# Tables without a scratch tile, angles one unit sooner, and an earlier load of x in a state-space layer on one core

## The chip, the cores and the metric

The kernel runs on one NeuronCore of a Trainium2 chip, in one launch. The metric is the device time of one execution in microseconds (us); the time of a kernel is the median of its runs. Engines are called PE (matrix), PEld (its weight loads), DVE (vector), ACT (scalar, activation functions), POOL (GpSimd) and SP (the queue that issues nearly all transfers here).

## The reference, cut to what matters

The program is one step of a decoder trunk: a state-space (S5) layer with a gated output, a convolutional FFN, a shared K/V projection, a differential attention layer and a second FFN, for a prompt of 1024 tokens and 8 x 8 sample tokens. The change lies in the first layer alone:

```
def s5_mixer(u, h0, lam_re, lam_im, log_dt, b_re, b_im, c_re, c_im, d_skip, w_glu):
    lam_dt = lam * dt;  lam_bar = exp(lam_dt);  b_bar = ((lam_bar - 1) / lam) * b
    # per group g (64 of them, 16 channels, 64 complex states), per token:
    #   h = lam_bar * h + b_bar @ u ;  y = real(c @ h)
    z = gelu(y + d_skip * u)
    gl = z @ w_glu
    return gl[..., :D] * sigmoid(gl[..., D:]), h_last
...
x = x + rmsnorm(s5_mixer(rmsnorm(x, a_pre_g), ...), a_post_g)
```

## The kernel before

**Layout.** `s5` cuts the 1024 tokens into 128 rows of 8 consecutive tokens. The recurrence inside a row is a product with small tables; between rows it is a real first-order scan over 128 steps on DVE, after the phase of each state was turned away by a table of cosines and sines. The 64 groups are handled in 8 blocks of 8 groups, each block in units of 3, 3 and 2 groups: 24 units, k = 3b + i for block b.

**Preparation** (L199 to L411, in a pool `s5prep`; its order on each engine is chosen by the framework's planner). It loads the parameters, b and c, transposes b, c and the powers of lambda (`bt`, `ct`, `NT`) with PE into the layouts `Yt` and `Dt`, and reads all of x (`xj`, eight transfers of 512 KB through four buffers) only to get the row norms: an ACT Square with a sum for each, then `rstd_from` on DVE, then `rs`.

**The block loop** is written out by hand (`tc.manual_schedule()`, L635 on): every engine runs its instructions in the order of the program text. The pieces are generators, and `run(...)` advances each by one stage:

- `load(b)`: x of one block into `zk` (three buffers); `scale(b)`: eight ACT multiplications by `rs` into `xg`, in two stages.
- `tables(b)`: six DVE operations on 128x1024 in three stages, which make `gn`, `cl` and `cw`; before, one product goes through a scratch tile `ax`. Two transfers follow (`cw<-cl`).
- `angles(q)`: for the two blocks 2q and 2q+1, three DVE operations on the same tile `ax` (stage 1), then ACT's Abs and three Sin and six transfers between partition halves (stage 2); the results are `cosT` and `sinT` of the two blocks. `ax` has one buffer. A tile is written again only when the readers of its former content, transfers among them, are done.
- `lags(b)`: 16 small products, four ACT copies, two POOL operations and seven transfers (L514) into `M1`.
- `turn(k)` and `states(k)`: PE transposes, POOL and ACT copies, 12 matmuls; `factors(k)`: one ACT copy into `Rs`; `scan(k)`: seven DVE operations that need `cosT`, `sinT`, `Rs` and the matmuls' PSUM; `out(k)`: PE products with `M1`, `cl`, `cw`; `gelu(k)`: ACT, and a store; `z_out(b)`: 8 PE transposes, two ACT casts and two DVE subtractions (L630) into the `xT_hi` and `xT_lo` of the dense part.

In step k the loop issues turn(k+2), the first stage of z_out, out(k), the products of lags, states(k+2), scan(k+1), the rest of z_out, gelu(k), factors(k+2), load, and then the stages of tables, scale and angles for later blocks. After the loop `then()` opens the dense part, which begins with the GLU's weights (`raw<-in_glu_w_dram`).

Of the kernel before, what the change touches and what calls it, by code (L numbers as in the profile page):

```python
# [20 lines left out]
P = 128  # L21
# [52 lines left out]
def trunk_kernel(ctx, tc, I, O):  # L74
# [7 lines left out]
    def nm(s):  # L82
        uid[0] += 1
        return f"{s}_{uid[0]}"
# [79 lines left out]
    def s5(then):  # L164
        with ExitStack() as c5:
# [33 lines left out]
            with tc.tile_pool(name="s5prep", bufs=1, reuse_waits="tile") as pr:  # L199

                def pt(shape, tag, dtype=F32):
                    return pr.tile(shape, dtype, tag=tag, name=tag)
# [13 lines left out]
                ht = pt([P, 4, 2, S], "ht")  # L216
                nc.sync.dma_start(adn[:, 0], I["a_pre_g"][0].rearrange("(g c) -> g c", c=C))
                nc.sync.dma_start(adn[:, 1], I["ssm_d"][0].rearrange("(g c) -> g c", c=C))
                for s, b_ in enumerate(("ssm_b_re", "ssm_b_im")):
                    nc.sync.dma_start(bt[:, s], I[b_][0])  # L220
                for s, c_ in enumerate(("ssm_c_re", "ssm_c_im")):
                    nc.sync.dma_start(ct[:, :, s, :], I[c_][0])
                for s, h_ in enumerate(("state_ssm_re", "state_ssm_im")):
                    nc.sync.dma_start(ht[:, :, s, :], I[h_][0].rearrange("(q b) g p -> (b g) q p", b=2))

                nc.sync.dma_start(gr, I["a_pre_g"][0].rearrange("(g c) -> g c", c=C).partition_broadcast(P))
                sq = pt([P, D], "sq", BF16)
                s1 = pt([TS, 1], "s1")
                A.activation(sq[0:TS], xs, AF.Square, accum_out=s1)

                r = rstd_from(pr, s1, 1, TS, "r1")
                A.mul(xs, xs, r[0:TS])
# [113 lines left out]
                    V.tensor_scalar(EX[:, 2, h], sn[q, 8], -1.0 if h == 0 else 1.0, None, op0=ALU.mult)  # L346
                    GP.tensor_copy(EX[:, 3, h], ph8[q])

                ss = pt([P, L], "ss")
                for j in range(L):  # L350
                    xj = pr.tile([P, D], F32, tag="xj", name=nm("xj"), bufs=4)
                    nc.sync.dma_start(xj, xp[:, j])
                    A.activation(sq, xj, AF.Square, accum_out=ss[:, j : j + 1])
                r = rstd_from(pr, ss, L, P, "r")
                GP.tensor_copy(rs, r)

# [79 lines left out]
            def angles(q):  # L436


                x = bt_("ax", 1)
                (t, sr), (t1, s1) = trig[2 * q], trig[2 * q + 1] = [[bt_(n, 3) for n in ("cosT", "sinT")]  # L440
                                                                    for _ in range(2)]
                V.tensor_tensor(x, bc(PH[:, q], 2, NCH), bc(kk, 1, BG), ALU.mult)
                V.tensor_scalar(t, x, MAGIC, None, op0=ALU.add)
                V.scalar_tensor_tensor(x, t, MAGIC, x, op0=ALU.subtract, op1=ALU.subtract)
                yield
                A.activation(t, x, AF.Abs)
                A.activation(sr, x, AF.Sin, scale=-TWO_PI)
                A.activation(x, x, AF.Sin, scale=TWO_PI)
                A.activation(t, t, AF.Sin, bias=halfpi, scale=-TWO_PI)
                lo, hi = slice(0, 64), slice(64, 128)  # L450
                for dst, i, src, j in ((t1, lo, t, hi), (t1, hi, t, hi), (s1, lo, sr, hi), (s1, hi, x, hi),
                                       (t, hi, t, lo), (sr, hi, x, lo)):
                    nc.sync.dma_start(dst[i], src[j])
                yield
# [16 lines left out]
            def tables(b):  # L471

                gs = slice(b * BG, (b + 1) * BG)

                def tb(w):
                    return Dt[:, w, :, gs].rearrange("p j g -> p g j").unsqueeze(3).broadcast_to([P, BG, L, C])

                def yb(w):
                    return Yt[:, w, gs].unsqueeze(2).broadcast_to([P, BG, L, C])

                gn, t = bt_("gn"), bt_("ax", 1)
                V.tensor_tensor(v4(gn), yb(0), tb(0), ALU.mult)
                V.tensor_tensor(v4(t), yb(1), tb(1), ALU.mult)
                yield
                V.tensor_tensor(gn, gn, t, ALU.add)
                cl = bt_("cl")
                V.tensor_tensor(v4(cl), yb(2), tb(2), ALU.mult)
                blocks[b].append(gn)
                yield
                cw = bt_("cw")  # L490
                V.tensor_tensor(v4(cw), yb(3), tb(3), ALU.mult)
                V.tensor_tensor(cl, cl, cw, ALU.add)
                blocks[b] += cl, cw
                nc.sync.dma_start(cw[0:64], cl[64:128])
                nc.sync.dma_start(cw[64:128], cl[0:64])
                yield
# [138 lines left out]
            with tc.manual_schedule():  # L635
                def run(*gs):
                    for g in gs:
                        next(g, None)

                for b in range(3):  # L640
                    load(b)
                tab, sca, lag, ang = tables(0), scale(0), lags(0), angles(0)
                run(sca, sca, tab, tab, ang)
                turn(0)
                run(ang, tab)
                factors(0)
                states(0)
                run(lag, lag)
                tab = tables(1)
                run(tab)  # L650
                for k in range(-1, nun):

                    b, i = k // 3, k % 3
                    if k + 2 < nun:
                        turn(k + 2)
                    zo = z_out(b - 1) if i == 0 and b else iter(())
                    run(zo)
                    if k >= 0:
                        out(k)
                    if i == 1 and b + 1 < NBK:  # L660
                        lag = lags(b + 1)
                        run(lag)
                    if k + 2 < nun:
                        states(k + 2)
                    if k + 1 < nun:
                        scan(k + 1)
                    run(zo, zo)
                    if k >= 0:
                        gelu(k)
                    if k + 2 < nun:  # L670
                        factors(k + 2)
                    if i == 0 and b and b + 2 < NBK:
                        load(b + 2)
                    if i == 1 and b + 1 < NBK:
                        run(lag)
                        if b + 2 < NBK:
                            tab = tables(b + 2)
                            run(tab)
                    if i == 2 and b + 2 < NBK:
                        sca = scale(b + 2)  # L680
                        run(sca, tab)
                        if b % 2 == 0:
                            ang = angles(b // 2 + 1)
                            run(ang)
                    if i == 0 and b + 1 < NBK:
                        run(sca, tab)
                        if b % 2 == 1:
                            run(ang)
                for _ in z_out(NBK - 1):
                    pass  # L690
            c5l.close()
# [1323 lines left out]
```

## Time and profile before

| what | value |
|---|---|
| median of 3 runs | 2748.95 us (2748.61 to 2752.87) |
| the profiled execution's own time | 2752.58 us |
| its span, first to last instruction | 2750.8 us |
| mean granted clock of PE | 0.972 |
| busy: PE / DVE / ACT / POOL | 2528.7 / 1953.1 / 1255.9 / 692.9 us |

The span lies 1.8 us inside the profiled execution's time, and that execution is 3.6 us above the median. The state-space layer takes the first 245 us or so; the first GLU matmul starts at 250.34 us. The table's shares are averages over all stages; the stage of the change has limits of its own.

### The profile page before, as it was taken

To read this page: it belongs to the slowest core of one execution; us is meant where nothing else is said; L and a number is where in the kernel's file an instruction comes from. 1 tells how busy PE (TensorE), PEld (TensorE's weight loads), DVE (VectorE), ACT (ScalarE), POOL (GpSimd) and SP (SyncE) were. 2 spreads that over 40 slices of the span, in tenths; PEclk is the share of its full clock that TensorE was granted. 3 is DMA by queue.
4 is the path that set the end of the run, shared out by engine and by line. 5 is a ranking of instruction groups with operands and counts; after the bars stand their busy time and mean duration, and the time that the engine had idled before them with its cause. 6 is when DMAs were issued, how large, how long until landed. Compare 5 with 4: busy or idle time off the path is not lost.

```text
span 2750.8 us, 39548 instructions
## 1 busy us (share of the span) xinstructions
PE 2528.7 (92%) x14362; PEld 2215.9 (81%) x14362; DVE 1953.1 (71%) x3719; ACT 1255.9 (46%) x2472; POOL 692.9 (25%) x943
## 2 busy tenths in 40 slices
PE   5777997999999989999999799999699999998995
PEld 4666886899999977778777688887599999996774
DVE  6885229776666789985222688865877776779998
ACT  5563124444444453444322577753444444454332
POOL 2221000111222266510201322100021222237661
PEclk9989998999999999999999999999899999999998
DMA  6334213222222243344656333324312222233324
GB/s 157 78 94 101 61 54 108 77 74 72 72 72 72 77 130 90 109 136 167 202 170 203 87 93 93 95 90 153 107 64 72 73 79 73 72 108 100 100 86 146
DMA packets 258023, 279.69 MB, mean 102 GB/s; under 512 B 41836, under 2 KB 205988, under 8 KB 257828
## 3 DMA queue, kind: packets, MB, share of 16 engines
q1 hardware_dynamic: 253508, 264.90, 31.4%
q0 software_dynamic: 3232, 10.29, 1.7%
q8 instruction: 114, 1.87, 0.3%
q10 hardware_dynamic: 1088, 1.97, 0.2%
q14 instruction: 81, 0.66, 0.1%
HBM read 187.82 MB, written 68.58 MB: 93 GB/s over the span
## 4 chain that ended last, share of the span: by engine, by line
PE 66%; DVE 16%; DMA 6%; ACT 5%; issue 4%; POOL 2%; SPq 1%; DVEq 0%; ACTq 0%; POOLq 0%
PE mm L784 18%; PE mm L785 18%; PE mm L786 18%; PE mm L1357 2%; DVE acc L1368 2%; DVE S L1830 1%; DVE xT_lo L137 1%; DMA raw<-in_w_down_dram 1%; DVE wst L137 1%; PE mm L1858 1%; DMA gr<-gd 1%; ACT S L1834 1%; PE tr L832 1%; DVE xT_hi L137 1%; DMA sinT<-sinT 1%
## 5 line engine op out<-in xcount | busy, mean ns | idle before, releaser
L784 PE MATMUL mm<-xT_hi,whi 128*128 128x320 f32 (+1 forms) x1408 | 459.6, 328 | 5.8 <-ACT xT_hi L136 2.8
L785 PE MATMUL mm<-xT_lo,whi 128*128 128x320 f32 (+1 forms) x1408 | 456.4, 324 | 0.1
L786 PE MATMUL mm<-xT_hi,wlo 128*128 128x384 f32 (+1 forms) x1408 | 454.8, 324 | 0.0
L1146 POOL COPY cvo<-acc 128x2 f32<-128x2 f32 x88 | 158.9, 1805 | 678.2 <-ACT acc L1129 678.2
L784 PEld LDWEIGHTS mm<-xT_hi,whi 128*128 128x128 f32 x1408 | 265.3, 189 | 15.0 <-DVE acc L1112 9.6
L137 DVE TENSOR_TENSOR wlo<-raw,whi 128x1024 fp32r<-128x1024 f32 x88 | 107.5, 1222 | 236.4 <-PE mm L785 231.9
L785 PEld LDWEIGHTS mm<-xT_lo,whi 128*128 128x128 f32 x1408 | 266.1, 189 | 0.9 <-DVE xT_lo L137 0.9
L786 PEld LDWEIGHTS mm<-xT_hi,wlo 128*128 128x128 f32 x1408 | 265.8, 189 | 0.2
L1143 DVE SCALAR_TENSOR_TENSOR acc<-acc,cpar,acc 128x1104 f32<-128x1104 f32 x176 | 240.5, 1387 | 0.7 <-ACT acc L1141 0.5
L784 PE MATMUL mm<-whi,xT_hi 128*128 128x512 f32 x576 | 228.3, 401 | 4.1 <-ACT whi L767 4.1
L785 PE MATMUL mm<-wlo,xT_hi 128*128 128x512 f32 x576 | 229.0, 398 | 0.0
L786 PE MATMUL mm<-whi,xT_lo 128*128 128x512 f32 x576 | 228.4, 398 | 0.0
L136 ACT CAST whi<-raw 128x1024 fp32r<-128x1024 f32 x88 | 92.8, 1055 | 283.6 <-PE mm L786 265.3
L1368 DVE TENSOR_TENSOR acc<-mm,acc 128x512 f32<-128x512 f32 x279 | 183.9, 679 | 9.2 <-PE mm L786 8.7
L784 PE MATMUL mm<-acc,whi 128*128 128x384 f32 x528 | 178.6, 339 | 3.8 <-DVE acc L1106 1.9
L786 PE MATMUL mm<-acc,wlo 128*128 128x384 f32 x528 | 178.7, 339 | 0.0
L785 PE MATMUL mm<-acc,whi 128*128 128x384 f32 x528 | 178.6, 338 | 0.0
L784 PEld LDWEIGHTS mm<-whi,xT_hi 128*128 128x128 f32 x576 | 108.8, 189 | 33.6 <-ACT whi L767 4.4
L786 PEld LDWEIGHTS mm<-whi,xT_lo 128*128 128x128 f32 x576 | 108.6, 189 | 26.6 <-issue 0.9
L785 PEld LDWEIGHTS mm<-wlo,xT_hi 128*128 128x128 f32 x576 | 108.6, 189 | 26.0 <-issue 0.4
L1141 ACT ACTIVATE acc<-acc,cpar 128x1104 f32<-128x1104 f32 x88 | 115.5, 1314 | 30.4 <-DVE acc L1112 19.8
L1830 DVE CUSTOM_DVE_ANT_0 S<-mm,tb 128x512 f32<-128x512 f32 (+3 forms) x192 | 101.2, 552 | 29.4 <-PE mm L1828 26.0
(559 smaller groups left out, 6263.6 us busy)
## 6 DMA issues: line engine op xcount, KB each, us to landing
raw<-in_w_up_dram SPq DMA_DIRECT2D x88, 512.0 KB
gd<-acc SPq DMA_DIRECT2D x44, 552.0 KB
raw<-in_w_down_dram SPq DMA_DIRECT2D x44, 512.0 KB
gr<-gd SPq DMA_DIRECT2D x80, 256.0 KB
raw<-in_glu_w_dram SPq DMA_DIRECT2D x32, 256.0 KB
acc<-in_cache_k_dram SPq DMA_DIRECT2D x16, 512.0 KB
acc<-in_cache_v_dram SPq DMA_DIRECT2D x16, 512.0 KB
xj<-in_x_prompt_dram SPq DMA_DIRECT2D x8, 512.0 KB
```

The lines of the kernel that those rows point to most:

```text
L136: A.copy(hi_ap, ps_ap)
L137: V.tensor_tensor(lo_ap, ps_ap, hi_ap.bitcast(F32), ALU.subtract)
L784: PE.matmul(out, lh, rh, start=start, stop=False, **kw)
L785: PE.matmul(out, lh, rl, start=False, stop=False, **kw)
L786: PE.matmul(out, ll, rh, start=False, stop=stop, **kw)
L832: PE.transpose(ps[:, c * n : (c + 1) * n], y[:, c * P : (c + 1) * P], ident[0:n, 0:n])
L1141: A.activation(hc, hb[:, 2 : 2 + TG], AF.Identity, bias=cp[:, ft, 3:4], scale=cp[:, ft, 2:3])
L1143: V.scalar_tensor_tensor(hc, hb[:, tap : tap + TG], cp[:, ft, tap : tap + 1], hc, op0=ALU.mult, op1=ALU.add)
L1146: GP.tensor_copy(co[:, 0:2], hb[:, SEQ : SEQ + 2])
L1357: PE.matmul(pa[h], lt, wt[:, h * 512 : (h + 1) * 512], start=st and j == 0, stop=sp and j == len(seq) - 1)
L1368: V.tensor_tensor(a, ps, a, ALU.add)
L1830: V.tensor_tensor_reduce(S_[j][:, k0 : k0 + w], ps[:, 0:w], H["tb"][:, b0 : b0 + w], 0.125, -3e38, ALU.add, ALU.max, mx[:, j, c : c + 1])
```

## The change

Six things change, all in `s5`:

1. In the preparation the transfers of `xj` are issued ahead of b and c (four at once, four more as buffers come free), and the transfers of the sample states `ht` after them.
2. `tables` no longer uses `ax`: the second product goes into `cl`, is added to `gn`, and `cl` is then written by the third product. Stage 1 has one DVE operation instead of two, stage 2 three instead of two.
3. `angles(0)` works in halves: Abs into a buffer of `zk`, then for each half of the partitions one cosine, one transfer and two Sin that write both halves themselves; two transfers in all instead of six.
4. `angles(q)` for q > 0 starts one unit sooner (stage 1 in unit 1 of an even block, stage 2 in unit 2).
5. `z_out` and `load` of odd blocks come one unit later.
6. At the loop's start angles go ahead of tables and scale; `factors(0)` goes behind `lags(0)`; `load(2)` behind both.

```diff
+                xj = [pr.tile([P, D], F32, tag="xj", name=nm("xj"), bufs=4) for _ in range(4)]
+                for j in range(4):
+                    nc.sync.dma_start(xj[j], xp[:, j])
                 for s, b_ in enumerate(("ssm_b_re", "ssm_b_im")):
                     nc.sync.dma_start(bt[:, s], I[b_][0])
...
-                for s, h_ in enumerate(("state_ssm_re", "state_ssm_im")):
-                    nc.sync.dma_start(ht[:, :, s, :], I[h_][0].rearrange("(q b) g p -> (b g) q p", b=2))
...
+                ss = pt([P, L], "ss")
+                for j in range(L):
+                    if j >= 4:
+                        xj.append(pr.tile([P, D], F32, tag="xj", name=nm("xj"), bufs=4))
+                        nc.sync.dma_start(xj[j], xp[:, j])
+                    A.activation(sq, xj[j], AF.Square, accum_out=ss[:, j : j + 1])
+                for s, h_ in enumerate(("state_ssm_re", "state_ssm_im")):
+                    nc.sync.dma_start(ht[:, :, s, :], I[h_][0].rearrange("(q b) g p -> (b g) q p", b=2))
...
-                ss = pt([P, L], "ss")
-                for j in range(L):
-                    xj = pr.tile([P, D], F32, tag="xj", name=nm("xj"), bufs=4)
-                    nc.sync.dma_start(xj, xp[:, j])
-                    A.activation(sq, xj, AF.Square, accum_out=ss[:, j : j + 1])
...
+                lo, hi = slice(0, 64), slice(64, 128)
+                if q == 0:
+
+                    xa = bt_("zk", 3)
+                    A.activation(xa, x, AF.Abs)
+                    for i, tc_, ts in ((lo, t, sr), (hi, t1, s1)):
+                        A.activation(tc_[i], xa[i], AF.Sin, bias=halfpi[i], scale=-TWO_PI)
+                        nc.sync.dma_start(tc_[hi if i == lo else lo], tc_[i])
+                        A.activation(ts[lo], x[i], AF.Sin, scale=-TWO_PI)
+                        A.activation(ts[hi], x[i], AF.Sin, scale=TWO_PI)
+                        yield
+                    return
...
-                gn, t = bt_("gn"), bt_("ax", 1)
+                gn = bt_("gn")
                 V.tensor_tensor(v4(gn), yb(0), tb(0), ALU.mult)
-                V.tensor_tensor(v4(t), yb(1), tb(1), ALU.mult)
                 yield
-                V.tensor_tensor(gn, gn, t, ALU.add)
                 cl = bt_("cl")
+                V.tensor_tensor(v4(cl), yb(1), tb(1), ALU.mult)
+                V.tensor_tensor(gn, gn, cl, ALU.add)
                 V.tensor_tensor(v4(cl), yb(2), tb(2), ALU.mult)
...
-                for b in range(3):
+                for b in range(2):
                     load(b)
                 tab, sca, lag, ang = tables(0), scale(0), lags(0), angles(0)
-                run(sca, sca, tab, tab, ang)
+                run(ang, tab, ang, sca, tab, sca)
                 turn(0)
-                run(ang, tab)
-                factors(0)
+                run(tab)
                 states(0)
                 run(lag, lag)
+                factors(0)
+                load(2)
                 tab = tables(1)
-                run(tab)
+                run(tab, ang)
...
-                    zo = z_out(b - 1) if i == 0 and b else iter(())
+                    zo = z_out(b - 1) if i == b % 2 and b > 0 else iter(())
...
-                    if i == 0 and b and b + 2 < NBK:
+                    if i == b % 2 and b > 0 and b + 2 < NBK:
                         load(b + 2)
...
                             tab = tables(b + 2)
                             run(tab)
+                            if b % 2 == 0:
+                                ang = angles(b // 2 + 1)
+                                run(ang)
                     if i == 2 and b + 2 < NBK:
                         sca = scale(b + 2)
                         run(sca, tab)
                         if b % 2 == 0:
-                            ang = angles(b // 2 + 1)
                             run(ang)
                     if i == 0 and b + 1 < NBK:
                         run(sca, tab)
-                        if b % 2 == 1:
-                            run(ang)
```

## Rows read from the trace of the kernel before

**Rows 1.** Busy time of each engine in three stretches of the block loop, each of two blocks (from unit 2 of blocks 0, 2 and 4); the columns are the stretch, its length, busy us (and instructions) of PE, PEld, DVE, ACT and POOL, the granted clock of PE, the DMA share and GB/s.
```profile
77.11:126.23 49.12, 36.80 (x324) 31.78 (x323) 40.60 (x62) 30.16 (x73) 9.13 (x23) 0.90 0.37 91
126.23:175.90 49.67, 34.62 (x298) 30.61 (x301) 40.27 (x62) 28.88 (x68) 10.61 (x22) 0.86 0.37 89
175.90:225.84 49.94, 35.27 (x316) 30.26 (x310) 41.46 (x62) 30.02 (x72) 10.60 (x22) 0.90 0.33 79
```

**Rows 2.** What DVE waited for between 60 and 262 us: line, releaser, us in total, times, longest.
```profile
DVE ax L483 <- DMA sinT<-ax: 34.3, 4, 11.3
DVE za L570 <- PE mm L551: 1.0, 1, 1.0
```

**Rows 3.** The timeline of DVE in the first two blocks of the loop: start, us, instruction, and in brackets the idle time before it.
```profile
79.85 1.42 DVE L482 TENSOR_TENSOR gn<-Yt,Dt 128x1024 f32<-128x1024 f32 x1
...
82.33 0.55 DVE L570 TENSOR_TENSOR za<-mm,cosT 128x384 f32<-128x384 f32 x1
...
86.01 1.22 DVE L485 TENSOR_TENSOR gn<-gn,ax 128x1024 f32<-128x1024 f32 x1
...
88.29 1.22 DVE L442 TENSOR_TENSOR ax<-PH,kk 128x1024 f32<-128x1024 f32 x1
...
91.41 0.55 DVE L570 TENSOR_TENSOR za<-mm,cosT 128x384 f32<-128x384 f32 x1
...
95.09 1.11 DVE L630 TENSOR_TENSOR xT_lo<-tr,xT_hi 128x512 fp32r<-128x512 f32 x1
...
97.10 1.22 DVE L491 TENSOR_TENSOR cw<-Yt,Dt 128x1024 f32<-128x1024 f32 x1
...
99.50 0.42 DVE L570 TENSOR_TENSOR za<-mm,cosT 128x256 f32<-128x256 f32 x1
...
102.25 1.42 DVE L482 TENSOR_TENSOR gn<-Yt,Dt 128x1024 f32<-128x1024 f32 x1
111.06 1.23 DVE L483 TENSOR_TENSOR ax<-Yt,Dt 128x1024 f32<-128x1024 f32 x1 [7.39 <-DMA sinT<-ax]
```

**Rows 4.** The timeline of ACT in the same blocks: the last scaling of unit 2 of block 0, and the first and last operation of stage 2 of `angles(1)`.
```profile
84.00 1.28 ACT L467 ACTIVATE xg<-zk,rs 128x128 f32<-128x128 f32 x4
...
95.13 1.05 ACT L446 ACTIVATE cosT<-ax 128x1024 f32<-128x1024 f32 x1
...
99.53 1.13 ACT L449 ACTIVATE cosT<-cosT,halfpi 128x1024 f32<-128x1024 f32 x1
```

**Rows 5.** The timeline of SP's queue: the first and the last issue of the transfers of `angles(1)`.
```profile
100.89 1.52 SPq L453 DMA_DIRECT2D cosT<-cosT  x2
...
107.44 0.46 SPq L453 DMA_DIRECT2D sinT<-ax  x1
```

**Rows 6.** The timeline of PE in the same blocks: half of the transposes of z_out(0), the start of out(3), and the states(5) behind it.
```profile
84.95 0.60 PE L622 MATMUL tr<-ident,zk 128*128 128x128 f32 x4
...
88.65 0.46 PE L593 MATMUL mm<-M,U 128*128 128x128 f32 x2 [2.67 <-DMA M<-M]
...
92.98 0.73 PE L551 MATMUL mm<-U,M 128*128 128x136 f32 x4
```

**Rows 7.** PE in a short stretch behind that wait: stretch, length, busy us (instructions), granted clock, DMA share, GB/s.
```profile
90.00:92.00 2.00, 2.00 (x10) 0.50 0.00 0
```

**Rows 8.** The timeline of DVE at the end of the preparation and the start of the loop.
```profile
38.78 0.17 DVE L118 TENSOR_SCALAR rv<-ss 128x8 f32<-128x8 f32 x1 [2.50 <-ACT sq L353]
...
41.01 1.23 DVE L482 TENSOR_TENSOR gn<-Yt,Dt 128x1024 f32<-128x1024 f32 x1
...
45.69 1.42 DVE L442 TENSOR_TENSOR ax<-PH,kk 128x1024 f32<-128x1024 f32 x1
...
63.93 1.22 DVE L483 TENSOR_TENSOR ax<-Yt,Dt 128x1024 f32<-128x1024 f32 x1 [11.30 <-DMA sinT<-ax]
```

**Rows 9.** The timeline of ACT at the start of the loop.
```profile
42.31 2.44 ACT L467 ACTIVATE xg<-zk,rs 128x128 f32<-128x128 f32 x8 [3.09 <-POOL rs L355]
...
49.13 1.06 ACT L446 ACTIVATE cosT<-ax 128x1024 f32<-128x1024 f32 x1 [2.04 <-DVE ax L444]
...
53.57 1.49 ACT L509 COPY M<-mm 16x256 f32<-16x256 f32 x4
```

**Rows 10.** The timeline of PE in the preparation (first transposes of b, last transposes) and at the start of the loop.
```profile
9.76 0.34 PE L367 MATMUL mm<-ident,bt 64*128 64x64 f32 x1 [9.76 <-DMA bt<-in_ssm_b_im_dram]
...
32.73 3.67 PE L399 MATMUL mm<-ident,NT 64*128 64x64 f32 x32 [0.85 <-ACT NT L336]
...
44.81 0.90 PE L531 MATMUL tr<-ident,xg 128*128 128x128 f32 x3 [7.37 <-ACT xg L467]
...
47.02 1.70 PE L551 MATMUL mm<-U,M 128*128 128x136 f32 x6 [0.66 <-ACT M L539]
48.51 1.49 PE L553 MATMUL mm<-U,M 128*128 128x128 f32 x6
51.63 1.05 PE L505 MATMUL mm<-cl,gn 128*16 128x128 f32 x16 [1.63 <-DVE cl L492]
```

**Rows 11.** Two stretches of 1 us, while c is loaded and while x is loaded; the columns as in rows 1 (the last two are the DMA share and GB/s).
```profile
11.00:12.00 1.00, 1.00 (x10) 0.65 (x8) 0.96 (x7) 0.56 (x1) 0.58 (x3) 1.00 1.41 153
...
17.00:18.00 1.00, 1.00 (x8) 0.69 (x6) 1.00 (x3) 1.00 (x1) 0.00 (x0) 1.00 1.02 414
```

**Rows 12.** SP's queue in the preparation: the issue of the first three transfers of x.
```profile
10.78 1.38 SPq L352 DMA_DIRECT2D xj<-in_x_prompt_dram  x3
```

More of the change, by code (lines that the diff above doesn't have):

```diff
@@ L449, in angles @@
                 A.activation(t, t, AF.Sin, bias=halfpi, scale=-TWO_PI)
-                lo, hi = slice(0, 64), slice(64, 128)
                 for dst, i, src, j in ((t1, lo, t, hi), (t1, hi, t, hi), (s1, lo, sr, hi), (s1, hi, x, hi),
```

## The prediction

> **What bounds the kernel now.** I read the busy times by stretch first, then DVE's waits, then the timelines of single engines. The page puts PE at 92% of the whole span, but in the block loop it is not the limit: over two blocks of 49.1 to 49.9 us DVE is busy 40.3 to 41.5 us, PE 34.6 to 36.8, ACT 29 to 30 [rows 1]. DVE has one wait there that counts: L483 writes `ax`, and the transfers of `angles` still read it, 34.3 us in four waits [rows 2]. One is 11.3 us at the loop's start [rows 8]; the others sum to 34.3 - 11.3 = 23.0 us, 7.4 us of it in the first pair of blocks [rows 3]. From 79.85 to 103.7 us DVE has no gap. So the loop is bound by DVE plus one stall for two blocks, and a us saved here should reach the end: what follows is a chain of matmuls that starts when the loop is done.
>
> **The three stalls in the loop.** First, what taking `ax` out of `tables` gives alone. The tables' six operations stay six, of the same shape, so DVE's work is unchanged. Without the wait L483 would run at 103.7 and unit 6's scan would want `cosT` and `sinT` at 104.8; they land where `ax` came free, near 111.0. The wait would move to the scan and 1.1 us would be gained. The earlier `angles` must bring the rest. I set unit 2's scan to zero (77.1 us before; 2.7 us ahead of 79.85 [rows 3]). DVE costs from rows 3: a scan of three groups 3.7 (82.33 to 86.01), of two 2.75 (99.50 to 102.25); two table operations 2.3 to 2.4 (86.01 to 88.29, 97.10 to 99.50), so some 1.2 each and 3.4 for three; angles 3.1 (88.29 to 91.41); the split 2.0 (95.09 to 97.10). After the change the order is: scan 2.7, table 1.4, angles 3.1 (ends 7.2); scan, three tables (14.3); scan, two tables (20.4); scan 2.75, split 2.0, one table (26.5); and then unit 6's scan. Stage 2 of `angles` runs on ACT behind unit 2's scaling, which began at 84.0 and took 1.2 [rows 4], so from 85.2, which is 8.1; its four operations and one table load take 5.5 (95.13 to 100.66 [rows 4]), to 13.6. From ACT's end to the landing took 111.0 - 100.7 = 10.4 before, since the six issues wait for each other and end at 107.44 [rows 4, 5]. So the tables of angles land at 24.0 and are wanted at 26.5. The wait goes, with 2.5 us in hand: 23.0 us for the three.
>
> What is late next? PE's out(3) waited for `M1` until 88.65, 11.5 after `cl` was ready at 77.1, and states(5) came 4.3 later, at 92.98, done by some 94.5 [rows 6]: 17.4 on this scale, wanted by unit 5's scan at 20.4. In the next block `cl` is ready at 20.4, two casts for the moved split (2 us on ACT) may stand ahead of the four lag copies, and states(8) end near 20.4 + 17.4 + 2 = 39.8, wanted at 41.7. Stage 2 on ACT (8.1 to 13.6) falls where ACT's next gelu would wait for out(3), which ends near 15.9 [rows 6]. SP is held for 6.5 us by the angles' issues (100.89 to 107.44 [rows 5]), but from 13.6 on: behind them stand the store of a gelu and the `cw` transfers, whose `cl` comes at 20.4. The load of odd blocks goes to SP one unit later, ahead of `M1`'s issues; it waits only for transposes that PE has run by then. The moved split holds a PSUM buffer in the unit that also needs one for lags, so states(6) may start only when a cast, a gelu or a lag copy frees one. I allow 0.5 us for each of three odd blocks (the nearest row is the single wait of a scan for PE, 1.0 us [rows 2]; bounds 0 and 1.6, where the states would follow the split's last subtraction): -1.5.
>
> **The tail.** For the last odd block the split of block 6 comes in unit 22. Its eight transposes, two groups of 0.6 that overlap a little [rows 6], used to lie in PE's wait for `M1`; now they stand ahead of out(22): -1.0 us, hidden in nothing.
>
> **The start.** Before, DVE waited for the last Square, did the row norms (38.78 to 41.0) and began tables at 41.01 [rows 8]. With x first the norms are done early, and what ends last is PE's chain that starts with b: from 9.76 to 32.73 + 3.67 = 36.4, of which 0.85 was a wait for `NT` that an emptier ACT removes [rows 10]. DVE's last copy leaves with that end. But b now stands behind 2.1 MB of x. While x flowed the rate was 414 GB/s, while c flowed 153 [rows 11]; 2.1 MB at 414 are 5.1 us, an upper bound for the delay since b's own issue is hidden in it; the lower bound is the four issues alone, 4 x 0.46 = 1.8 [rows 12]. I take 4.0, nearer to the upper, because one queue carries all of them. So DVE begins angles at 36.4 - 0.85 + 4.0 = 39.5 (37.3 to 40.7).
>
> From there, in us after that start: angles 3.4 (45.69 to 49.13 [rows 8, 9]); Abs, one cosine and two Sin of about 1.05 each, to 7.6 (a Sin on half the partitions is not in the trace; I take the full price, since the free size is the same, and half of it would gain 1.6); scaling 2.4, to 10.0; transposes and copies 2.2 (44.81 to 47.02), to 12.2; states 3.0 (47.02 to 50.0), to 15.2; the 16 lag products 1.05 [rows 10] and four copies 1.5 [rows 9], to 17.7; then `factors(0)`, moved behind them, 0.4, to 18.1. Only then can unit 0's scan step run. The rest of that unit is 2.0, three tables 3.4: 23.5. Unit 1 needs the three Sin of the other half (to 21.3), copies (22.4) and states (25.3); its scan ends at 28.3, two tables at 30.7, and unit 2 starts at 31, when states(2) come behind out(0). Before, unit 2 started at 77.1. So 77.1 - (39.5 + 31) = 6.6 us gained. With PE quick throughout and half-price Sin the walk is 28, with another wait for PE 33: bounds 77.1 - 65.3 = 11.8 and 77.1 - 73.7 = 3.4.
>
> The Trainium skill, "DMA: Bandwidth & Descriptors", section "Queues, rings and completion order", says that on each DMA engine descriptors are consumed in ring order. By that rule b waits for all of x: the start is 5.1 late, not 4.0, and the sum 1.1 us less; if the engines served both alike it would be late by the issues alone and 2.2 us more. Nothing in this trace has the two loads in that order.
>
> **The sum.** 23.0 + 6.6 - 1.0 - 1.5 = 27.1 us. On the profiled execution's 2752.6 that is 2725.5. The median lies 3.6 below that execution, so the median after is 2748.95 - 27.1 = about 2722 us, 1.0% faster. Its own range is 2715 (start at 11.8, no small waits: 23.0 + 11.8 - 1.0 = 33.8) to 2730 (start 3.4, 1.6 for each of four odd blocks: 19 gained).
>
> **The rivals.**
> (a) The stall only changes its name. The margin of the angles is 2.5 us and that of the states 2 to 3; if PSUM buffers, a zk load of the next block (half a MB beside the same transfers) or SP's order costs 5 us more at these places, 2.5 us or so comes back in each of six blocks, 15 us: gain 12, 2737. For it: the transfers took 10.4 us where ACT needed 5.5, and waits in SP lengthen each other [rows 4, 5]. Against: before, DVE was gapless for 24 us with the same PE and ACT work [rows 3].
> (b) No change that can be measured (within 0.2%, 5.5 us, about what a measurement of this kernel can tell). The angles land as late as before relative to the scan, because stage 2 waits on ACT behind a late gelu: then the 23 us shrink to 1.1 x 3 = 3.3 and the start's 6.6 lose the tail's and the small waits' 2.5, 7.4 in all; with a start at the lower bound 4.2, 2745. For it: ACT runs strictly behind out(k). Against: ACT's scaling was over at 85.2 [rows 4], well before out(3) began.
> (c) Slower. PE becomes the bound at its lower clock. Behind a wait of 2.67 us its granted clock was 0.50, which is 1.2 of 2.4 GHz, and out(3) took 4.3 us [rows 6, 7]. A pair of blocks is 36.8 x 0.90 = 33 us of PE at full clock [rows 1]; at a mean clock of 0.60 it would take 55 us, 6 more than now: three pairs cost 18, less the start's 6.6: 2760. It decides from a mean of 0.65 down (33 / 0.65 = 51, which eats the start's gain). Against: the clock was 0.86 to 0.90 with the waits in it, and the change shortens waits. The Trainium skill, "TensorE: Matmul & The Clock Gate", Part 1, says that the throttled clock is the default and activity releases it; by that the loop gets warmer, and the rows, where 0.50 follows a wait, agree.
> (d) More than 35 us: b is not delayed and PE regroups its transposes.
>
> **How the numbers follow.** My forecast 0.60, (a) 0.20, (b) 0.07, (c) 0.07, (d) 0.06. 2722 is that of the likeliest. The range 2712 to 2738 takes in the forecast and (a) and leaves out 0.2. Faster by over 0.2% holds the forecast, (a) and (d): 0.86; same 0.07; slower 0.07.
>
> **What the profile after would show.** Right: no wait of DVE for a transfer of `ax` or `sinT`; DVE busy over 95% of a pair, which takes about 42.5 us; the first transposes of b near 13.8 instead of 9.76; DVE's angles from 39.5, unit 2's scan near 70.5; the first GLU matmul near 223 instead of 250.3. Wrong: a wait of L570 for `cosT` or `sinT` (a), of L570 for PE's L551 beyond 1.6 us (a, or c with a clock below 0.65), or transposes of b after 17 us, which would put the start where it was. A planner that orders the dense part anew could shift the rest by a few us; no row here prices that.

## The result, and the profile after

The kernel after takes 2736.47 us (median of 5, 2734.39 to 2739.58) against 2751.81 for the kernel before beside it: ratio 0.9946 (95%: 0.9932 to 0.9961). Timed once more later it took 2730.78 against 2753.36: 0.9920 (0.9906 to 0.9933). So it is faster, as forecast, but by 15 to 23 us instead of 27.1. The profiled executions, from which the rest is read, are 2752.58 and 2735.75 us: 16.8 gained.

The kernel after in the three stretches that answer to [rows 1], columns as there:

```profile
77.23:120.86 43.63, 34.60 (x326) 31.74 (x325) 40.94 (x62) 30.80 (x73) 11.44 (x22) 0.92 0.42 102
120.86:163.04 42.18, 31.67 (x320) 27.63 (x319) 40.91 (x62) 30.69 (x73) 9.48 (x23) 1.00 0.44 105
163.04:205.58 42.54, 33.96 (x304) 30.05 (x304) 40.92 (x62) 29.86 (x70) 10.28 (x22) 0.92 0.39 92
```

And all that DVE waited for in them (line, releaser, us in total, times, longest), which answers to [rows 2]:

```profile
DVE za L585 <- PE mm L566: 1.3, 1, 1.3
DVE E L592 <- ACT zs L628: 0.5, 1, 0.5
```

The waits for transfers are gone, DVE is busy 94 to 97% of a pair, and a pair of blocks takes 42.2 to 43.6 us instead of 49.1 to 50.3. (Before, unit 2 of block 4 starts at 176.50, 0.6 later than where [rows 1] cut, so that its second and third pair took 50.3 and 49.3.) (L570, L551, L577, L593 and L442 of before are L585, L566, L592, L608 and L446 here.)

The start, on PE and DVE; the lines answer to [rows 8, 10]:

```profile
15.47 0.34 PE L371 MATMUL mm<-ident,bt 64*128 64x64 f32 x1 [15.47 <-DMA bt<-in_ssm_b_im_dram]
...
39.79 3.62 PE L403 MATMUL mm<-ident,NT 64*128 64x64 f32 x32
```

```profile
43.94 0.68 DVE L404 COPY Dt<-mm 128x512 f32<-128x512 f32 x1
44.54 0.15 DVE L126 SCALAR_TENSOR_TENSOR rr<-rs,rr 128x8 f32<-128x8 f32 x1
44.61 1.21 DVE L446 TENSOR_TENSOR ax<-PH,kk 128x1024 f32<-128x1024 f32 x1
45.86 2.54 DVE L447 TENSOR_SCALAR cosT<-ax 128x1024 f32<-128x1024 f32 x1
...
77.23 0.42 DVE L585 TENSOR_TENSOR za<-mm,cosT 128x256 f32<-128x256 f32 x1
```

b's transposes begin 5.7 us later than before, angles at 44.61, and unit 2 starts at 77.23 where it started at 77.1 before: the start gained nothing.

The tail, on PE, and two stretches of it (stretch, length, busy of PE, PEld, DVE, ACT, POOL, granted clock, DMA share, GB/s). First the kernel before at the same place, the start of out(21) behind its wait for `M`:

```profile
235.48 0.46 PE L593 MATMUL mm<-M,U 128*128 128x128 f32 x2 [1.80 <-DMA M<-M]
```

```profile
236.00:238.00 2.00, 2.00 (x25) 1.88 (x26) 2.00 (x3) 0.00 (x0) 0.23 (x2) 1.00 0.03 8
```

Then the kernel after:

```profile
215.19 0.77 PE L608 MATMUL mm<-M,U 128*128 128x128 f32 x2 [2.73 <-DMA M<-M]
...
220.57 0.60 PE L637 MATMUL tr<-ident,zk 128*128 128x128 f32 x4
```

```profile
215.00:217.00 2.00, 1.81 (x8) 1.84 (x9) 0.78 (x2) 0.00 (x0) 0.00 (x0) 0.54 0.09 25
217.00:219.00 2.00, 2.00 (x14) 1.88 (x12) 0.00 (x0) 0.00 (x0) 0.10 (x2) 0.60 0.00 0
```

The account of the profiled executions, before to after: start (to unit 2) 77.11 to 77.23, -0.1 gained; loop 148.73 to 128.35, 20.4 gained; tail, to the first GLU matmul, 24.50 to 27.01, 2.5 lost. That matmul moves from 250.34 to 232.59, by 17.75. What follows it, called the dense part below, takes 2500.5 before and 2501.4 after.

The state-space part of the kernel after ran, unchanged, in three more profiled executions (e5, e9, e10 below). Over the four, unit 2 started at 77.1 to 78.1, the loop took 126.5 to 128.6 us, the tail 25.9 to 27.0, and the first GLU matmul came at 230.84 to 232.59. So a difference of under 2 us between two single executions cannot be told from that spread.

### The profile page after: what moved, and what is told of

The parts are those of the page before. It is cut to its first block, busy times and chain, and to the rows that moved or that the text cites. A ratio compares the mean times of both kernels' runs of the same rounds, so it can differ in the third digit from the quotient of the medians.

```text
span 2734.0 us, 39538 instructions
## 1 busy us (share of the span) xinstructions
PE 2519.4 (92%) x14362; PEld 2208.4 (81%) x14362; DVE 1957.0 (72%) x3719; ACT 1260.9 (46%) x2475; POOL 694.3 (25%) x943
## 4 chain that ended last, share of the span: by engine, by line
PE 38%; DVE 9%; DMA 3%; ACT 3%; issue 2%; POOL 1%; SPq 0%; DVEq 0%; POOLq 0%; ACTq 0%
PE mm L800 11%; PE mm L801 10%; PE mm L802 10%; DVE S L1846 1%; ACT S L1850 1%; PE mm L1373 1%; DVE acc L1384 1%; DVE S L1860 1%; PE mm L1874 1%; DMA gr<-gd 1%; PE tr L848 1%; DVE qx L1789 1%; DMA raw<-in_w_down_dram 1%; DMA raw<-in_w_v_dram 1%; POOL xr L1265 0%
```

## The experiments

The table gives each profiled execution: its time, the first GLU matmul, the dense part (span less that), and the mean distance of the 22 blocks of layer 1's up-projection, from the first and last start of the product that closes a block.

| kernel | us | first GLU | dense part | block |
|---|---|---|---|---|
| before | 2752.58 | 250.34 | 2500.5 | 22.60 |
| after | 2735.75 | 232.59 | 2501.4 | 22.61 |
| e1 x behind b and c | 2718.15 | 227.40 | 2489.0 | 22.28 |
| e2 b and c, then x | 2730.27 | 229.34 | 2499.1 | 22.62 |
| e3 split back | 2736.05 | 232.71 | 2501.6 | 22.58 |
| e4 tables alone | 2741.57 | 250.12 | 2489.7 | 22.34 |
| e5 other dense order | 2730.27 | 232.38 | 2496.1 | 22.34 |
| e6 e1 and tail | 2730.61 | 226.66 | 2502.1 | 22.54 |
| e7 fills on ACT | 2726.80 | 229.46 | 2495.5 | 22.55 |
| e8 together | 2715.58 | 223.91 | 2489.9 | 22.28 |
| e9 after again | 2730.78 | 231.28 | 2497.7 | 22.53 |
| e10 as e5 | 2727.24 | 230.84 | 2494.7 | 22.33 |
| e11 as e1 | 2725.08 | 227.85 | 2495.5 | 22.34 |
| e12 e1, other dense order | 2728.89 | 227.26 | 2499.8 | 22.62 |

**The place of x (e1, e2).** In the changed kernel, e1 puts the transfers of x and their Squares back where they were:

```diff
-                xj = [pr.tile([P, D], F32, tag="xj", name=nm("xj"), bufs=4) for _ in range(4)]
-                for j in range(4):
-                    nc.sync.dma_start(xj[j], xp[:, j])
...
+                for j in range(L):
+                    xj = pr.tile([P, D], F32, tag="xj", name=nm("xj"), bufs=4)
+                    nc.sync.dma_start(xj, xp[:, j])
+                    A.activation(sq, xj, AF.Square, accum_out=ss[:, j : j + 1])
                 r = rstd_from(pr, ss, L, P, "r")
```

> The changed kernel with its first edit undone: x, its Squares and the sample states are loaded where they were before. Theory (x ahead of b costs the start, because b's rows come behind 2.1 MB of x and mixed with c's small rows, and because the planner no longer groups c's transposes): PE's first transposes of b at 9.8 us instead of 15.5, its last transposes done near 36.4 instead of 43.4, DVE's angles from 41 (after the row norms, whose last Square ends at 38.6) instead of 44.6, unit 2's scan near 73.6 instead of 77.2, the first GLU matmul near 229 instead of 232.6. Rival (the order of the loads does not matter, the norms after the last Square hold the start as long as b did): angles near 44.6 again and the first GLU matmul within 1 us of 232.6.

Measured, PE and DVE of e1:

```profile
9.79 0.34 PE L367 MATMUL mm<-ident,bt 64*128 64x64 f32 x1 [9.79 <-DMA bt<-in_ssm_b_im_dram]
...
32.80 3.67 PE L399 MATMUL mm<-ident,NT 64*128 64x64 f32 x32 [0.86 <-ACT NT L336]
```

```profile
40.86 0.17 DVE L126 SCALAR_TENSOR_TENSOR rr<-rs,rr 128x8 f32<-128x8 f32 x1
40.95 1.22 DVE L442 TENSOR_TENSOR ax<-PH,kk 128x1024 f32<-128x1024 f32 x1
42.20 2.54 DVE L443 TENSOR_SCALAR cosT<-ax 128x1024 f32<-128x1024 f32 x1
...
73.80 0.42 DVE L581 TENSOR_TENSOR za<-mm,cosT 128x256 f32<-128x256 f32 x1
```

PE's chain is that of before to 0.1 us, angles start at 40.95 and unit 2 at 73.80, 3.4 sooner than in the kernel after: loading x ahead costs the start 3.4 us. (Over all executions with the start of either, unit 2 starts at 77.1 to 78.1 with x ahead and at 73.8 to 74.0 with x behind.) The time fell by more than the 5.2 us of the first GLU matmul; the dense part was shorter too, which no theory had.

e2 loads b, c and the gains first, then four of x, with the Squares early:

```diff
-                for j in range(4):
-                    nc.sync.dma_start(xj[j], xp[:, j])
                 for s, b_ in enumerate(("ssm_b_re", "ssm_b_im")):
...
                 nc.sync.dma_start(gr, I["a_pre_g"][0].rearrange("(g c) -> g c", c=C).partition_broadcast(P))
+                for j in range(4):
+                    nc.sync.dma_start(xj[j], xp[:, j])
```

> The changed kernel with b, c and the gain's broadcast issued first and the four transfers of x right behind them; Squares as early as in the changed kernel. Theory (only b's delay was wrong about the first edit; early norms are worth having): b's transposes at 9.8, PE's preparation done by 36 to 38, norms done before that, DVE's angles from 36 to 38, the first GLU matmul at 224 to 226. Rival (x behind c's small rows comes as late as before, so the norms hold the start): angles from 41 on, the first GLU matmul at 229, as with x behind.

DVE of e2:

```profile
40.54 0.17 DVE L118 TENSOR_SCALAR rv<-ss 128x8 f32<-128x8 f32 x1 [1.34 <-ACT sq L236]
...
42.66 1.23 DVE L446 TENSOR_TENSOR ax<-PH,kk 128x1024 f32<-128x1024 f32 x1
```

b's transposes begin at 9.81, but angles at 42.66: now the last Square (ACT) holds up the row norms, and these stand ahead of the angles in DVE's order although the angles need none of them. PE's last transposes begin at 34.63, 1.8 later than in e1 with the same b. So the rival held: the norms hold the start, and the first GLU matmul came at 229.34. In the orders tried, whichever load comes second ends the preparation, x by way of the norms, b by way of PE.

**The moved split (e3)**, with `z_out` and `load` of odd blocks back at the first unit:

```diff
-                    zo = z_out(b - 1) if i == b % 2 and b > 0 else iter(())
+                    zo = z_out(b - 1) if i == 0 and b > 0 else iter(())
...
-                    if i == b % 2 and b > 0 and b + 2 < NBK:
+                    if i == 0 and b > 0 and b + 2 < NBK:
```

> The changed kernel with the split and the load of odd blocks back at unit 0. Theory (the moved split costs the tail: eight transposes of 1.0 us ahead of out(22), and 1.5 us because out(21) runs at the lower clock behind a longer wait of PE): from unit 2's scan of block 6 to the first GLU matmul 24.5 us as before, not 27.0, while a pair of blocks still takes 42 to 43.6: the first GLU matmul near 230.1. Rival (the loop needs the moved split, or its waits come back): a pair takes 44 us or more and the first GLU matmul is at 232.6 or later.

The first pair of blocks took 45.29 us instead of 43.63, the other two 42.36 and 42.72. DVE's wait of e3 between 77 and 206 us (columns as above):

```profile
DVE za L585 <- PE mm L566: 3.0, 1, 3.0
```

The tail shrank from 27.01 to 24.58 (208.13 to 232.71). So the loop is 2.0 us longer without the moved split and the tail 2.4 shorter; unit 2 started 0.5 later, and the first GLU matmul came at 232.71 against 232.59. That is what the rival said, and this part of the change is worth nothing that can be seen; the 2.0 us of the loop are themselves no more than it varies by (126.5 to 128.6 with the split moved).

**The tables alone (e4)**, in the kernel before:

```diff
-                gn, t = bt_("gn"), bt_("ax", 1)
+                gn = bt_("gn")
...
-                V.tensor_tensor(v4(t), yb(1), tb(1), ALU.mult)
                 yield
-                V.tensor_tensor(gn, gn, t, ALU.add)
                 cl = bt_("cl")
+                V.tensor_tensor(v4(cl), yb(1), tb(1), ALU.mult)
+                V.tensor_tensor(gn, gn, cl, ALU.add)
```

> The kernel before with one edit alone: tables without the scratch tile; angles, splits and loads stay. Theory (the transfers of angles are as late as the scratch tile was): the wait moves from the tables' second product to the scan's wait for sinT or cosT, of about 6 to 7 us in each pair of blocks; 1.1 us are gained for each pair and 1.1 at the start, 4.4 in all: the first GLU matmul near 246. Rival (the scratch tile was the whole stall): no wait over 2 us is left, the first GLU matmul near 227 to 230.

DVE's waits of e4 (columns as above) between 60 and 262 us:

```profile
DVE za L570 <- DMA cosT<-cosT: 29.7, 4, 10.3
...
DVE zb L571 <- DMA sinT<-ax: 2.3, 4, 0.8
```

32.0 us against the 34.3 of [rows 2]: the wait went to the scan, as argued, and the first GLU matmul came 0.2 us sooner, not 4.4. Taking `ax` out of the tables is nothing by itself; the angles one unit sooner make the gain. They could not have come sooner with `ax` left in: by the program text they would then write it between the two operations of `tables` that write and read it. Again the dense part was 11 us shorter.

**The length of the dense part (e5).** Before, after, e2 and e3 have blocks of 22.6 us, e1 and e4 of 22.3. The framework orders the instructions of each engine by a simulated run of the whole program; in that order DVE's steps of one block of layer 1 stand in one sequence in before, after, e2 and e3, and in others in e1 and e4. Call the first order A, the others B; B is two sequences, one in e4, e5 and e10, another in e1, e8 and e11. Four memsets of a tile on DVE (0.98 us each) at the start of layer 1's feed-forward turn A into B with the state-space part as it is:

```diff
         tail.gain = None
+        if i == 1:
+            t = slot("acc")
+            V.memset(t, 0.0)
+            V.memset(t, 0.0)
+            V.memset(t, 0.0)
+            V.memset(t, 0.0)
```

> The changed kernel with four memsets of one 128-row tile of the dense part on VectorE added at the start of layer 1's feed-forward; the state-space part is left as it is. In the planner's order that comes out, VectorE's sequence within each of layer 1's blocks is that of the tables-only run and no longer that of the changed kernel. Theory (the 11 us that two earlier runs gained in the dense part come from the order that the planner wrote for layer 1's up-projection): first GLU matmul at 232.6 as in the changed kernel, blocks of layer 1 every 22.3 us instead of 22.6, dense part 2490 to 2494 with the added memsets, time 2725 to 2729. Rival (the dense part is shorter for what the state-space part left behind, not for its own order): dense part 2501 to 2505, time 2736 to 2740.

Blocks of 22.34, dense part 2496.1, time 2730.27: the block was as expected; the gain in the dense part, 5.3 us, was less than the 7 to 11 expected.

**The tail (e6)**, on top of e1:

```diff
-                    zo = z_out(b - 1) if i == b % 2 and b > 0 else iter(())
+                    zo = z_out(b - 1) if i == (b % 2 if b + 1 < NBK else 0) and b > 0 else iter(())
```

> The run with x behind b and c again, and the last odd block's output work back at the pair's first unit (the other odd blocks keep the moved split). The planner's order of layer 1's blocks is that of the changed kernel again. Order theory: state-space part 2.5 us shorter (first GLU matmul at 224.9 against 227.4, the tail after the last pair 24.5 instead of 27.0), but blocks of layer 1 every 22.6 us and a dense part of 2500, so 2726 to 2728: slower than the run with x behind alone. Rival (the order in which x is loaded makes the dense part shorter): dense part 2489, time 2715 to 2716. Rival on the tail: the last pair loses to transfers what the tail gains, and the first GLU matmul stays at 227.

The first GLU matmul came at 226.66, 0.7 sooner than in e1, not 2.5. The planner's order was A, the blocks took 22.54 us, and the kernel 2730.61: with a quicker state-space part 12.5 us slower than e1. The tail gave so little because e1's out(21) ran in 2.7 us at a granted clock of 1.00, as in the kernel before; only the 0.9 us of the transposes ahead of out(22) were left to win.

**The slow range reduction (e7).** In the kernel after, the second operation of `angles(0)` (L447, the range reduction) took 2.54 us, in later blocks 0.69 to 0.78. GpSimd's two zero fills of `M` ran beside it; e7 gives them to ACT.

```diff
             for t in M1s:
-                GP.memset(t, 0.0)
+                A.mul(t, Yt[:, 0].rearrange("p (a g) c -> p a (g c)", a=BG), 0.0)
```

> The changed kernel with the two zero fills of M done by ScalarE instead of GpSimd. Theory (the range reduction of the angles took 2.54 us instead of 0.69 because GpSimd's fills ran beside it): 0.7 us for it, the first scan of unit 2 at about 75.4 instead of 77.2, first GLU matmul at about 230.8, time about 2734 (the planner's order of layer 1's blocks is that of the changed kernel). Rival (it is slow by itself, for instance because its input has just been written): 2.5 us again, first scan of unit 2 at 77.2 and 2736.

DVE in e7:

```profile
44.62 1.21 DVE L446 TENSOR_TENSOR ax<-PH,kk 128x1024 f32<-128x1024 f32 x1
45.86 0.78 DVE L447 TENSOR_SCALAR cosT<-ax 128x1024 f32<-128x1024 f32 x1
...
75.84 0.41 DVE L585 TENSOR_TENSOR za<-mm,cosT 128x256 f32<-128x256 f32 x1
```

0.78 instead of 2.54, and unit 2 1.4 us sooner: GpSimd's fills were the cause. The first GLU matmul came 3.1 us sooner, as the first pair lost its wait for PE too; e9 and e10 lost that wait without this edit, so only the 1.4 us are the fills'. The time, 2726.80, is 9 below after's, of which 6 lie in the dense part with order A; that much can lie between two executions of one kernel (below).

**All together (e8):** e1, e6 and e7, and `factors(0)` ahead of `states(0)`:

```diff
-                states(0)
-                run(lag, lag)
-                factors(0)
+                factors(0)
+                states(0)
+                run(lag, lag)
```

> All that the runs point to, together: x behind b and c again, M's zero fills on ScalarE, the first block's factors ahead of its states, the last odd block's output work at the pair's first unit; the rest of the change stays. The planner's order of layer 1's blocks is the one of the run with x behind. If the terms add up: start 1.8 less, tail 2.5 less, factors 1.4 less than the 227.4 of the run with x behind, so the first GLU matmul at 221.7 to 223, dense part 2489, time 2711 to 2713, ratio to the kernel before 0.985. Rival (the gains hide each other, or ScalarE's fills delay the angles' sines): 2715 to 2718.

2716.26 us (median of 4, 2712.86 to 2721.51), ratio 0.9869 (0.9852 to 0.9886); unit 2 at 71.38, first GLU matmul at 223.91. It beats both kernels. The first GLU matmul is 3.5 us sooner than in e1, where the terms were summed to 5.7: of the 2.2 missing, 0.8 are the start's (2.4 gained of 3.2) and 1.5 the tail's (25.7 us against e1's 26.7, 1.0 gained of 2.5). The time is in the rival's range.

**x and the order, crossed (e9 to e12).** e9 is the changed kernel, e10 is e5, e11 is e1, and e12 is e1 with one memset at the start of layer 0, which makes layer 1's order A:

```diff
+        if i == 0:
+            t = slot("acc")
+            V.memset(t, 0.0)
```

> The changed kernel once more, as one of four that cross the place of x with the planner's order of layer 1's blocks: x ahead of b and c, the order of the kernel before (call it A, blocks every 22.6 us). Single executions of one kernel have been seen to spread by 5 to 9 us, so that one look at each is too little for the differences asked after. Both theories: 2736, ratio to the kernel before 0.994.

> The changed kernel with four memsets of one tile (0.98 us of VectorE each) at the start of layer 1's feed-forward, with which the planner writes the other order of layer 1's blocks (B, one every 22.3 us). Theory (the order is worth 22 blocks by 0.3 us, so 6 us, whatever stands before it): 6 us less than the changed kernel with order A, 2730, or up to 4 more where the memsets are not hidden. Rival (the order is worth nothing, what single looks showed was the spread of executions): 2736 to 2740, as with order A or slower by the memsets.

> The changed kernel with x behind b and c again; the planner's order is B. Theory: first GLU matmul 5.2 us sooner than in the changed kernel (one look showed 227.4 against 232.6) and 6 us from the order: 11 us less than x ahead with order A, 2725, and 5 less than x ahead with order B; one look showed 2718. Rival (the order is worth nothing): 2731.

> The same with one memset of a tile (0.98 us of VectorE) at the start of layer 0's feed-forward, with which the planner writes order A in layer 1. Theory: the 5.2 us of the start stay, the 6 us of the order are lost: 2731, 6 more than x behind with order B and 5 less than x ahead with order A. Rival (the order is worth nothing): the same as x behind with order B within 1 us.

| | order A | order B |
|---|---|---|
| x ahead | 2730.78, ratio 0.9920 (0.9906 to 0.9933) | 2729.15, 0.9911 (0.9898 to 0.9925) |
| x behind | 2732.01, 0.9925 (0.9911 to 0.9938) | 2721.86, 0.9886 (0.9871 to 0.9902) |

The blocks repeat: 22.53 and 22.62 with A, 22.33 and 22.34 with B, and in all fourteen executions of the first table 22.53 to 22.62 with A and 22.28 to 22.34 with B. A stretch of 300 us of layer 1, first of e9, then of e11 (columns as in the windows above; the count behind PE's busy time is its matmuls):

```profile
2131.00:2431.00 300.00, 298.58 (x1805) 293.37 (x1804) 213.11 (x243) 131.89 (x183) 82.41 (x104) 1.00 0.24 76
```

```profile
2128.00:2428.00 300.00, 300.00 (x1831) 298.74 (x1830) 219.46 (x246) 131.99 (x187) 35.63 (x111) 1.00 0.24 76
```

The closing products of the blocks (duration ns min/median/max, first and last start), first of e9, then of e11:

```profile
L1170 DVE TENSOR_TENSOR acc<-acc,acc x22: 1294/1300/1302, 1990.1 to 2463.2; 128x1104 f32<-128x1104 f32 x22
```

```profile
L1166 DVE TENSOR_TENSOR acc<-acc,acc x22: 1293/1300/1308, 1988.4 to 2457.6; 128x1104 f32<-128x1104 f32 x22
```

With B 1831 matmuls pass in the time of 1805. Over 21 distances (473.1 and 469.2 us here, 475.0 in e12) that is 4 to 6 us. In whole times the order was worth 10.2 us with x behind (the intervals lie apart) and 1.6 with x ahead, where the four memsets may have cost up to 3.9; x behind was worth 7.3 with B and nothing with A, although the first GLU matmul came 3 to 4 us sooner in both. The rival, that the order is worth nothing, falls for x behind; that the two effects simply add, as expected, was not shown. One reason is that order B is not the same sequence with x ahead (e10) and behind (e11). Another is in the table: the same kernel's dense part was 2501.4 and 2497.7 (after, e9) and 2489.0 and 2495.5 (e1, e11). It differs by up to 6.5 us from one execution to another.

What in order A costs the 0.2 to 0.3 us of a block stays open. The trace names 1.2 us of PE's waits for DVE in the 300 us of e9, and up to 1.8 more for POOL in others, where with B (e1, e10, e11) PE waits for nothing. That is part of the 3 to 4 us that 300 us lose with A.

## Why the prediction was right or wrong

**Sign, mechanism and loop: right.** The 23.0 less 1.5 us were 20.4. No wait of DVE for `ax` or `sinT` is left, a pair takes 42.2 to 43.6 us (42.5 forecast), and the wait for PE that was feared came once, 1.3 us. e4 shows the step behind it: without the earlier angles the stall only moves to the scan. The range of 2712 to 2738 held both medians. Rival (a) gave nearly the time that came first, 2737, but not for its reason: the stall did not come back.

**The start: wrong, 6.6 us forecast, -0.1 measured.** This is the term that failed, in three places.
- "I take 4.0" for b behind x: b's transposes came 15.47 - 9.76 = 5.7 later, above the 5.1 called an upper bound. That bound priced all of x at 414 GB/s, the rate of one good stretch. x reached 434, but over the 6 us from 6 to 12, nearly all of them x, the mean was 373, at which 2.1 MB take 5.6. What followed was no slower than before: 178 GB/s for the 3.47 us up to b's transposes, against 202 for 3.76 us in the kernel before. The kernel after, then the kernel before:

```profile
8.00:9.00 1.00, 0.00 (x0) 0.00 (x0) 1.00 (x10) 0.40 (x1) 0.19 (x1) 1.00 1.06 434
...
6.00:12.00 6.00, 0.00 (x0) 0.00 (x0) 5.06 (x31) 4.32 (x7) 2.28 (x6) 1.00 0.98 373
12.00:15.47 3.47, 0.00 (x1) 0.04 (x1) 3.37 (x8) 2.52 (x6) 1.94 (x3) 1.00 1.16 178
```

```profile
6.00:9.76 3.76, 0.00 (x1) 0.03 (x1) 2.64 (x18) 1.15 (x2) 0.92 (x2) 1.00 1.07 202
```

  By the Trainium skill, "DMA: Bandwidth & Descriptors", "Queues, rings and completion order", whose ring order was weighed at 5.1, b waits for all of x; the trace agrees, since 5.7 is about what all of x took.
- "DVE's last copy leaves with that end", 0.85 us after PE's gain on `NT`: half of PE's transposes of c, which ran in large groups before (8 and 32 of a kind), now ran nearly all in turns of 1 and 4, and all of c took from 27.23 to 38.06, 10.8 us instead of 8.6. The last group began at 39.79 and ended at 43.4, 7.0 later than before where 4.0 - 0.85 = 3.15 was forecast, and DVE began angles 1.2 behind that end. Angles at 44.61 instead of 39.5: 5.1 us, of which b makes 1.7, c 2.2 and the wait behind PE 1.2.
- "angles 3.4" took 5.0, since L447 was held up by the fills (e7). The rest of the walk was right: 77.23 - 44.61 = 32.6, less that 1.65, is 31.0, as forecast.

5.1 + 1.65 is the whole miss. e1 shows that 3.4 of it are the price of x ahead of b, and e2 that b, c and then x does not free both PE's chain and the norms either.

**The tail: -1.0 forecast, -2.5 measured.** The transposes did move ahead of out(22). But they had also kept PE busy in its wait for `M`: PE waited 1.80 at 235.48 before and 2.73 now, and behind that its granted clock was 0.54 and 0.60, near the lower of its two levels (1.2 of 2.4 GHz), where it was 1.00 before. So out(21), up to the states behind it, took 4.4 us instead of 2.75: 1.6 of the 2.5, and the transposes are the other 0.9. That is what [rows 7] had shown in the loop and the step had not priced. Undoing it shortened the tail by 2.4 us in e3. It is not paid in each execution: in e9, the same kernel, PE's clock was low ahead of the wait (0.66 from 206 to 211), out(21) took 2.7 us at 1.00, and the tail 25.94.

Together: 6.7 us missing at the start, 1.5 in the tail and 1.1 in the loop make the 9.3 between 27.1 and the 17.75 by which the first GLU matmul moved.

**"A planner that orders the dense part anew could shift the rest by a few us; no row here prices that."** Between before and after it did not: both have order A, 0.9 us apart. But order B was 4 to 7 us away all along (22 blocks by 0.2 to 0.3).

## What to carry to other kernels

When a load is moved ahead, ask what it pushes back, and price that at the mean rate of the load in front, from its first byte to its last; here x gained nothing by being first, since the transposes behind b, which had ended 2.4 us ahead of the last Square, then ended 7.0 us later. Where a planner orders all engines by a simulated run, an edit in one stage can rewrite a stage a millisecond later: compare the length of the untouched stages before a difference of some us is put down to the edit. And time both kernels more than once, as the same program's untouched part moved by up to 6.5 us here.

## What the runs showed of the hardware that was not expected

A fill on GpSimd holds up some VectorE instructions and not others. The range reduction on SBUF, 128x1024 f32, takes 0.69 to 0.78 us, and 2.54 where GpSimd's two fills of M ran; 45.86 + 2.54 - 0.78 = 47.62 is about when the fills were over:

```profile
45.82 1.85 POOL L435 MEMSET M<- 128x1024 f32 x2
```

In the kernel before, the same fills (42.22 to 44.0) ran beside two-input products, which took their usual 1.22 and 1.23 us. The other way round, GpSimd's copy of 128x2 elements in the feed-forward, which takes 0.18 us at the least (88 copies in the kernel after), took 3.62 us beside DVE operations with two SBUF inputs; it ended as DVE went to an operand from PSUM (POOL, then DVE):

```profile
2329.19 3.62 POOL L1162 COPY cvo<-acc 128x2 f32<-128x2 f32 x1 [2.80 <-ACT acc L1145]
```

```profile
2329.20 1.22 DVE L137 TENSOR_TENSOR wlo<-xr,whi 128x1024 fp32r<-128x1024 f32 x1
2330.33 1.30 DVE L1170 TENSOR_TENSOR acc<-acc,acc 128x1104 f32<-128x1104 f32 x1
2331.55 1.22 DVE L137 TENSOR_TENSOR wlo<-xr,whi 128x1024 fp32r<-128x1024 f32 x1
2332.69 0.55 DVE L1122 TENSOR_TENSOR acc<-mm,acc 128x384 f32<-128x384 f32 x1
```

The Trainium skill, "SBUF — State Buffer", "SBUF: two separate sides", says that the two engines share a pair of ports under an exclusive lock: a VectorE operation in a two-port mode contends with any GpSimd operation, one with two SBUF inputs only with a GpSimd operation that reads SBUF. All three observations agree with it. The lock is said to be held for one instruction; here VectorE stayed out for both fills, and GpSimd for the three operations shown.
